# Row gather, running sum and projection: pairs of tiles handled as one, and gathers at most 7 pairs ahead

## The chip, the cores and the metric

One core of one Trainium2 chip. The metric is the device time of the core in microseconds (us), over a few executions on the same chip, and every kernel that is compared with another was timed in alternation with the kernel before on one chip. Beside it stands the span of one profiled execution. The engines go by their short names: PE multiplies matrices (PEld is its loading of weights), DVE, ACT and POOL work on elements, SP issues the stores. PSUM is the memory into which PE writes; to drain a PSUM tile is to copy it out to SBUF.

## The reference

```python
B, S, N, D = 16, 4096, 2048, 512          # x: fp32 (B,S,D); indices: (B,N), sorted, no repeats; w: fp32 (D,D)
gathered = x[np.arange(B)[:, None], indices, :]
cs = np.cumsum(gathered, axis=1)
out = np.matmul(cs, w).astype(np.float32)
```

## The kernel before

The 16 x 2,048 gathered rows are worked through as 256 tiles of 128 rows. A tile goes this way: POOL issues one indexed gather (128 rows of 2 KB, one index per partition) into a buffer; ACT casts it to fp16; PE multiplies it by a triangular matrix, which gives sums within the tile, into PSUM (`pa`); DVE adds the last column of the tile before and writes `csT`; PE multiplies that by `w16` into PSUM (`pb`); ACT or DVE drains `pb` to `ob`; SP stores two tiles at once.

```python
R, AHEAD = 2, 44
gp   = ctx.enter_context(tc.tile_pool(name="gp", bufs=AHEAD + 4))      # gathered rows: 48 tiles
g16p = ...bufs=6;  csp = ...bufs=5;  outp = ...bufs=10
psA  = ...bufs=3 (PSUM);  psB = ...bufs=5 (PSUM)
# ... (indices, w, the triangular matrix ut are loaded and built here) ...

def gather(t):
    g32s[t] = gp.tile([P, D], FP32, name="g32")
    ...
    nc.gpsimd.indirect_dma_start(out=g32s[t][:], out_offset=None, in_=x_flat,
        in_offset=bass.IndirectOffsetOnAxis(ap=ap, axis=0), element_offset=(t // NT) * S * D)

def cast(t):
    g16s[t] = g16p.tile([P, D], FP16, name="g16")
    nc.scalar.copy(out=g16s[t][:], in_=g32s.pop(t)[:])

# cumsum_tile(t): 4 matmuls into pa, then one add (or copy) on DVE into csT
# project_tile(t): 4 matmuls into pb, then
    if r == 0: nc.vector.tensor_copy(out=obs[g][:, r, :], in_=pb[:])
    else:      nc.scalar.copy(out=obs[g][:, r, :], in_=pb[:])
    # ... and after the second tile of a pair one store from SP

for t in range(FIRST, AHEAD): gather(t)          # 44 tiles of gathers before anything else
...
for t in range(T + LAG):
    if t + AHEAD < T: gather(t + AHEAD)
    if t + 1 < T:     cast(t + 1)
    if t < T:         cumsum_tile(t)
    if t >= LAG:      project_tile(t - LAG)
```

Of the kernel before, what the change touches and what calls it, by code (L numbers as in the profile page):

```python
# [1 line left out]

# [5 lines left out]

P = 128
FP32 = mybir.dt.float32  # L10
FP16 = mybir.dt.float16
U32 = mybir.dt.uint32


@with_exitstack
def kernel(
    ctx: ExitStack,
    tc: tile.TileContext,
    x: bass.AP,
    indices: bass.AP,  # L20
    w: bass.AP,
    out: bass.AP,
):
    nc = tc.nc

    B, S, D = x.shape
    N = indices.shape[1]
    R = 2
    Q = P // R
    DC = D // P  # L30
    NT = N // P
    T = B * NT
    FIRST = 2
    AHEAD = 44
    assert D == 512 and N % (R * P) == 0 and T % P == 0

    x_flat = x.rearrange("b s d -> (b s) d")

    const = ctx.enter_context(tc.tile_pool(name="const", bufs=1))
    gp = ctx.enter_context(tc.tile_pool(name="gp", bufs=AHEAD + 4))  # L40
    g16p = ctx.enter_context(tc.tile_pool(name="g16p", bufs=6))
    csp = ctx.enter_context(tc.tile_pool(name="csp", bufs=5))
    outp = ctx.enter_context(tc.tile_pool(name="outp", bufs=10))
    psA = ctx.enter_context(tc.tile_pool(name="psA", bufs=3, space=bass.MemoryType.PSUM))
    psB = ctx.enter_context(tc.tile_pool(name="psB", bufs=5, space=bass.MemoryType.PSUM))
    ctx.enter_context(tc.manual_schedule())


    idx_first = const.tile([P, FIRST, 2], U32)
    with nc.allow_non_contiguous_dma(reason="a few indices, one per partition"):  # L50
        nc.sync.dma_start(
            out=idx_first[:],
            in_=indices[0, 0 : FIRST * P].bitcast(U32).rearrange("(t p w) -> p t w", p=P, w=2),
        )

    KI = T // P
    idx_rows = indices.bitcast(U32).rearrange("b (t q) -> (b t) q", q=2 * P)
    idx64 = const.tile([P, KI, 2 * P], U32)
    for k in range(KI):
        nc.sync.dma_start(out=idx64[:, k, :], in_=idx_rows[k * P : (k + 1) * P, :])  # L60
    w32 = const.tile([P, DC, D], FP32)
    nc.sync.dma_start(out=w32[:], in_=w.rearrange("(c p) d -> p c d", p=P))


    ut = const.tile([P, R, Q], FP16)
    nc.gpsimd.memset(ut[:], 1.0)  # L66
    nc.gpsimd.affine_select(  # L67
        out=ut[:],
        in_=ut[:],
        compare_op=mybir.AluOpType.is_ge,  # L70
        fill=0.0,
        base=0,
        pattern=[[1, R], [R, Q]],
        channel_multiplier=-1,
    )
    ident = const.tile([P, P], FP32)
    make_identity(nc, ident[:])

    idxf = const.tile([P, KI, P], FP32)
    idxg = const.tile([P, KI, P], U32)  # L80
    w16 = const.tile([P, DC, D], FP16)

    g32s, g16s, cst, obs = {}, {}, {}, {}

    def gather(t):
        g32s[t] = gp.tile([P, D], FP32, name="g32")
        ap = idx_first[:, t, 0:1] if t < FIRST else idxg[:, t // P, t % P : t % P + 1]
        nc.gpsimd.indirect_dma_start(  # L88
            out=g32s[t][:],
            out_offset=None,  # L90
            in_=x_flat,
            in_offset=bass.IndirectOffsetOnAxis(ap=ap, axis=0),
            element_offset=(t // NT) * S * D,
        )

    def cast(t):
        g16s[t] = g16p.tile([P, D], FP16, name="g16")
        nc.scalar.copy(out=g16s[t][:], in_=g32s.pop(t)[:])  # L98

    def cumsum_tile(t):  # L100
        g, r = divmod(t, R)
        if r == 0:
            cst[g] = csp.tile([P, DC, R, P], FP16, name="csT")
        csT = cst[g]
        g16 = g16s.pop(t)
        pa = psA.tile([P, DC, R, Q], FP32, name="pa")
        for c in range(DC):
            nc.tensor.matmul(  # L108
                out=pa[:, c],
                lhsT=g16[:, c * P : (c + 1) * P],  # L110
                rhs=ut[:],
                start=(c == 0),
                stop=(c == DC - 1),
            )
        dst = csT[:, :, :, r * Q : (r + 1) * Q]
        if t % NT == 0:
            nc.vector.tensor_copy(out=dst, in_=pa[:])  # L117
            return
        if r == 0:
            last = cst[g - 1][:, :, R - 1, P - 1 : P]  # L120
        else:
            last = csT[:, :, R - 1, r * Q - 1 : r * Q]
        nc.vector.tensor_tensor(  # L123
            out=dst,
            in0=pa[:],
            in1=last.unsqueeze(2).broadcast_to([P, DC, R, Q]),
            op=mybir.AluOpType.add,
        )

    def project_tile(t):  # L130
        g, r = divmod(t, R)
        if r == 0:
            obs[g] = outp.tile([P, R, D], FP32, name="ob")
        csT = cst[g]
        pb = psB.tile([P, D], FP32, name="pb")
        for c in range(DC):
            nc.tensor.matmul(  # L137
                out=pb[:],
                lhsT=csT[:, c, r, :],
                rhs=w16[:, c, :],  # L140
                start=(c == 0),
                stop=(c == DC - 1),
            )
        if r == 0:
            nc.vector.tensor_copy(out=obs[g][:, r, :], in_=pb[:])  # L145
        else:
            nc.scalar.copy(out=obs[g][:, r, :], in_=pb[:])  # L147
        if r == R - 1:
            b, h = divmod(g, NT // R)
            dst = out[b, h * R * P : (h + 1) * R * P, :].rearrange("(p j) d -> p j d", j=R)  # L150
            nc.sync.dma_start(out=dst, in_=obs.pop(g)[:])

    for t in range(FIRST):
        gather(t)
    for k in range(KI):
        nc.vector.tensor_copy(out=idxf[:, k, :], in_=idx64[:, k, 0::2])  # L156
        idx_ps = psB.tile([P, P], FP32, name="idx_ps", tag="pb")
        nc.tensor.transpose(out=idx_ps[:], in_=idxf[:, k, :], identity=ident[:])  # L158
        nc.vector.tensor_copy(out=idxg[:, k, :], in_=idx_ps[:])  # L159
    for t in range(FIRST, AHEAD):  # L160
        gather(t)
    nc.scalar.copy(out=w16[:], in_=w32[:])  # L162

    LAG = R
    cast(0)
    for t in range(T + LAG):
        if t + AHEAD < T:
            gather(t + AHEAD)
        if t + 1 < T:
            cast(t + 1)  # L170
        if t < T:
            cumsum_tile(t)
        if t >= LAG:
            project_tile(t - LAG)


# [1 line left out]
_INS = ['x', 'indices', 'w']  # L178
_OUTS = [((16, 2048, 512), 'float32')]


# [23 lines left out]
```

## Time and profile before

| | before |
|---|---|
| time, median of 3 (lowest to highest) | 496.83 us (494.12 to 497.37) |
| profiled span (that run took 494.51 us) | 492.8 us |
| busy: PE / DVE / ACT / POOL | 68% / 52% / 43% / 49% of the span |
| DMA | 135.96 MB, mean 276 GB/s |
| start of the cast of tile 10 | 80.1 us |
| tiles 64 to 200, from cast to cast | 1.714 us each |

No engine is busy more than 68% of the time, so a table of totals doesn't say what the bound is. The groups of instructions show what the change touches on ACT and DVE (columns: line, engine, operation, output and input, count, then busy time and mean nanoseconds of one, then the idle time in front of them and what ended most of it):

```profile
L147 ACT COPY ob<-pb 128x512 f32<-128x512 f32 x128 | 74.9, 585 | 271.5 <-remote 147.2
...
L98 ACT CAST g<-g 128x512 f16<-128x512 f32 x256 | 145.7, 620 | 0.0
...
L145 DVE COPY ob<-pb 128x512 f32<-128x512 f32 x128 | 88.4, 691 | 76.2 <-PE pb L137 32.9
```

ACT's drains are the group to look at: 75 us of work with 271 us of standing still in front of it.

### The profile page before, as it was taken

The page shows a single profiled execution, that of the slowest core. Times are in us where ns is not written, and L with a number is a line of the kernel's source. Part 1 is how long each engine was busy: PE and PEld are TensorE (multiplying, and loading weights), DVE is VectorE, ACT ScalarE, POOL GpSimd, SP SyncE. Part 2 cuts the span into 40 slices and gives each one's busy share as a digit, 9 for nine tenths or more (in the row PEclk, how much of TensorE's full clock was granted, in tenths as well). Part 3 has the DMA queues.
Part 4 walks back from the last instruction along what each step waited for, and adds up shares of the span by engine and source line. Part 5 has one row for each costly group of instructions (what it writes and reads, how often), then busy time and mean ns, then how long its engine had stood idle before and what let it go on. Part 6 is the DMA issues. An engine that isn't in the chain of part 4 may idle for free. (4 is left out here: it accounts for less than half of the span.)

```text
span 492.8 us, 6383 instructions
## 1 busy us (share of the span) xinstructions
PE 334.8 (68%) x2050; PEld 162.4 (33%) x2050; DVE 256.3 (52%) x388; ACT 210.7 (43%) x386; POOL 243.2 (49%) x264
## 2 busy tenths in 40 slices
PE   2512012877777776788788776688886659799995
PEld 1201001433333333344333333344433324344442
DVE  1300000654665475456555664556665656577774
ACT  4100001443554454355444453535554444566663
POOL 6777771544555645564555555556555555300000
PEclk9956555787999999798888998988899997999999
DMA  7878773688888989888898988988998997855555
GB/s 235 252 206 256 208 212 122 221 293 295 304 306 299 330 321 319 291 292 282 293 320 313 345 300 301 322 274 305 308 339 310 306 335 254 319 212 211 213 211 204
DMA packets 40035, 135.96 MB, mean 276 GB/s; under 512 B 6465, under 2 KB 6721, under 8 KB 40001
## 3 DMA queue, kind: packets, MB, share of 16 engines
q0 software_dynamic: 20480, 67.13, 44.3%
q1 hardware_dynamic: 19520, 68.43, 35.0%
q8 instruction: 16, 0.26, 0.2%
q14 instruction: 19, 0.15, 0.1%
HBM read 68.42 MB, written 67.11 MB: 275 GB/s over the span
## 5 line engine op out<-in xcount | busy, mean ns | idle before, releaser
L137 PE MATMUL pb<-w,csT 128*128 128x512 f16 x1024 | 290.9, 411 | 115.9 <-DVE csT L123 72.0
L88 POOL DMA_INDIRECT g<-in_x_dram,idxg x254 | 240.0, 945 | 180.9 <-ACT g L98 122.1
L123 DVE TENSOR_TENSOR csT<-pa,csT 128x512 f16<-128x512 f32 x240 | 165.0, 688 | 138.0 <-PE pa L108 65.0
L147 ACT COPY ob<-pb 128x512 f32<-128x512 f32 x128 | 74.9, 585 | 271.5 <-remote 147.2
L137 PEld LDWEIGHTS <-csT 128*128 128x128 f16 x1024 | 91.4, 104 | 205.2 <-DVE csT L123 89.6
L98 ACT CAST g<-g 128x512 f16<-128x512 f32 x256 | 145.7, 620 | 0.0
L108 PE MATMUL pa<-ut,g 128*128 128x128 f16 x1024 | 105.9, 230 | 33.4 <-ACT g L98 22.2
L145 DVE COPY ob<-pb 128x512 f32<-128x512 f32 x128 | 88.4, 691 | 76.2 <-PE pb L137 32.9
L108 PEld LDWEIGHTS <-g 128*128 128x128 f16 x1024 | 76.9, 103 | 115.7 <-ACT g L98 57.4
L117 DVE CAST csT<-pa 128x512 f16<-128x512 f32 x16 | 11.0, 690 | 13.2 <-PE pa L108 7.6
L162 ACT CAST w<-w 128x2048 f16<-128x2048 f32 x1 | 1.9, 1897 | 6.0 <-DMA w<-in_w_dram 6.0
L158 PE MATMUL idx_ps<-ident,idxf 128*128 128x128 f32 x2 | 0.9, 461 | 4.3 <-DVE idxf L156 4.3
L88 POOL DMA_INDIRECT g<-in_x_dram,idx_first x2 | 2.0, 1022 | 1.4 <-DMA idx_first<-in_indices_dram 1.0
L156 DVE CAST idxf<-idx 128x128 f32<-128x128 uint32 x2 | 0.4, 222 | 3.5 <-DMA idx<-in_indices_dram 3.5
L158 PEld LDWEIGHTS idx_ps<-ident,idxf 128*128 128x128 f32 x2 | 0.4, 182 | 4.6 <-issue 3.8
L162 ACT ACT_TABLE_LOAD x1 | 1.3, 1283 | 0.8 <-PEq L189 0.8
L159 DVE CAST idxg<-idx_ps 128x128 uint32<-128x128 f32 x2 | 0.6, 292 | 1.2 <-PE idx_ps L158 1.2
L66 POOL MEMSET ut<- 128x128 f16 x1 | 0.2, 205 | 0.3 <-POOLq L189 0.3
L67 POOL TENSOR_SCALAR_AFFINE_SELECT ut<-ut 128x128 f16<-128x128 f16 x1 | 0.3, 292 | 0.1
masks.py:199 POOL TENSOR_SCALAR_AFFINE_SELECT ident<-ident 128x128 f32<-128x128 f32 x1 | 0.3, 292 | 0.1
L189 POOL MEMSET const-float32-0.0<- 128x1 f32 x1 | 0.1, 98 | 0.3 <-issue 0.3
masks.py:197 POOL MEMSET ident<- 128x128 f32 x1 | 0.2, 198 | 0.0
(3 smaller groups left out, 0.3 us busy)
## 6 DMA issues: line engine op xcount, KB each, us to landing
out_dram<-ob SPq DMA_DIRECT2D x128, 512.0 KB
g<-in_x_dram,idxg POOLq DMA_INDIRECT x254
w<-in_w_dram SPq DMA_DIRECT2D x1, 1024.0 KB
idx<-in_indices_dram SPq DMA_DIRECT2D x2, 128.0 KB
g<-in_x_dram,idx_first POOLq DMA_INDIRECT x2
idx_first<-in_indices_dram SPq DMA_DIRECT2D x1, 2.0 KB
```

Source lines behind the costliest of these rows:

```text
L88: nc.gpsimd.indirect_dma_start(out=g32s[t][:], out_offset=None, in_=x_flat, in_offset=bass.IndirectOffsetOnAxis(ap=ap, axis=0), element_of ...
L98: nc.scalar.copy(out=g16s[t][:], in_=g32s.pop(t)[:])
L108: nc.tensor.matmul(out=pa[:, c], lhsT=g16[:, c * P : (c + 1) * P], rhs=ut[:], start=(c == 0), stop=(c == DC - 1),)
L117: nc.vector.tensor_copy(out=dst, in_=pa[:])
L123: nc.vector.tensor_tensor(out=dst, in0=pa[:], in1=last.unsqueeze(2).broadcast_to([P, DC, R, Q]), op=mybir.AluOpType.add,)
L137: nc.tensor.matmul(out=pb[:], lhsT=csT[:, c, r, :], rhs=w16[:, c, :], start=(c == 0), stop=(c == DC - 1),)
L145: nc.vector.tensor_copy(out=obs[g][:, r, :], in_=pb[:])
L147: nc.scalar.copy(out=obs[g][:, r, :], in_=pb[:])
L156: nc.vector.tensor_copy(out=idxf[:, k, :], in_=idx64[:, k, 0::2])
L158: nc.tensor.transpose(out=idx_ps[:], in_=idxf[:, k, :], identity=ident[:])
L159: nc.vector.tensor_copy(out=idxg[:, k, :], in_=idx_ps[:])
L162: nc.scalar.copy(out=w16[:], in_=w32[:])
```

## The change

The intent: halve the number of instructions and of waits between engines by doing a cast, a drain and a PSUM tile for two tiles at once (part of an instruction's time doesn't grow with its length: ACT's cast of 512 elements took 620 ns in the trace before and its one cast of 2,048 1,897, so some 194 ns by the line through both, an estimate), and free memory by gathering fewer tiles ahead. The gathers themselves stay one per tile. Cut to its core:

```diff
-    AHEAD = 44                                   # tiles
+    AHEAD = 7                                    # pairs
-    gp = ...bufs=AHEAD + 4      # 48 buffers of one tile
+    gp = ...bufs=AHEAD + 1      # 8 buffers of a pair: 16 tiles
-    g16p 6, csp 5, psA 3, psB 5
+    g16p 3, csp 4, psA 2, psB 2                  # each now holds a pair
     def gather(g):
+        g32s[g] = gp.tile([P, R, D], FP32, name="g32")
+        for r in range(R):  # one indirect_dma_start per tile, as before
     def cast(g):
+        nc.scalar.copy(out=g16s[g][:], in_=g32s.pop(g)[:])      # [P, R, D]
     def cumsum(g):
+        # 8 matmuls into one pa, then two adds on DVE
     def project(g):
+        # 8 matmuls into one pb, then one drain:
+        if g % 4 == 3: nc.vector.tensor_copy(out=ob[:], in_=pb[:])
+        else:          nc.scalar.copy(out=ob[:], in_=pb[:])
+        # one store per pair, as before
     for g in range(G):
+        if g + AHEAD < G: gather(g + AHEAD)
+        if g + 2 < G:     cast(g + 2)            # two pairs ahead
+        if g + 1 < G:     cumsum(g + 1)
+        project(g)
```

More of the change, by code (lines that the diff above doesn't have):

```diff
@@ L32 @@
     T = B * NT
-    FIRST = 2
-    AHEAD = 44
+    G = T // R
+    GB = NT // R
+    FIRST = R
+    AHEAD = 7
     assert D == 512 and N % (R * P) == 0 and T % P == 0
@@ L39 @@
     const = ctx.enter_context(tc.tile_pool(name="const", bufs=1))
-    gp = ctx.enter_context(tc.tile_pool(name="gp", bufs=AHEAD + 4))
-    g16p = ctx.enter_context(tc.tile_pool(name="g16p", bufs=6))
-    csp = ctx.enter_context(tc.tile_pool(name="csp", bufs=5))
+    gp = ctx.enter_context(tc.tile_pool(name="gp", bufs=AHEAD + 1))
+    g16p = ctx.enter_context(tc.tile_pool(name="g16p", bufs=3))
+    csp = ctx.enter_context(tc.tile_pool(name="csp", bufs=4))
     outp = ctx.enter_context(tc.tile_pool(name="outp", bufs=10))
-    psA = ctx.enter_context(tc.tile_pool(name="psA", bufs=3, space=bass.MemoryType.PSUM))
-    psB = ctx.enter_context(tc.tile_pool(name="psB", bufs=5, space=bass.MemoryType.PSUM))
+    psA = ctx.enter_context(tc.tile_pool(name="psA", bufs=2, space=bass.MemoryType.PSUM))
+    psB = ctx.enter_context(tc.tile_pool(name="psB", bufs=2, space=bass.MemoryType.PSUM))
     ctx.enter_context(tc.manual_schedule())
@@ L81 @@
     w16 = const.tile([P, DC, D], FP16)
-    g32s, g16s, cst, obs = {}, {}, {}, {}
-    def gather(t):
-        g32s[t] = gp.tile([P, D], FP32, name="g32")
-        ap = idx_first[:, t, 0:1] if t < FIRST else idxg[:, t // P, t % P : t % P + 1]
-        nc.gpsimd.indirect_dma_start(
-            out=g32s[t][:],
-            out_offset=None,
-            in_=x_flat,
-            in_offset=bass.IndirectOffsetOnAxis(ap=ap, axis=0),
-            element_offset=(t // NT) * S * D,
-        )
-    def cast(t):
-        g16s[t] = g16p.tile([P, D], FP16, name="g16")
-        nc.scalar.copy(out=g16s[t][:], in_=g32s.pop(t)[:])
@@ L100, in cumsum_tile @@
-    def cumsum_tile(t):
-        g, r = divmod(t, R)
-        if r == 0:
-            cst[g] = csp.tile([P, DC, R, P], FP16, name="csT")
-        csT = cst[g]
-        g16 = g16s.pop(t)
-        pa = psA.tile([P, DC, R, Q], FP32, name="pa")
-        for c in range(DC):
-            nc.tensor.matmul(
-                out=pa[:, c],
-                lhsT=g16[:, c * P : (c + 1) * P],
-                rhs=ut[:],
-                start=(c == 0),
-                stop=(c == DC - 1),
-            )
-        dst = csT[:, :, :, r * Q : (r + 1) * Q]
-        if t % NT == 0:
-            nc.vector.tensor_copy(out=dst, in_=pa[:])
-            return
-        if r == 0:
-            last = cst[g - 1][:, :, R - 1, P - 1 : P]
-        else:
-            last = csT[:, :, R - 1, r * Q - 1 : r * Q]
-        nc.vector.tensor_tensor(
-            out=dst,
-            in0=pa[:],
-            in1=last.unsqueeze(2).broadcast_to([P, DC, R, Q]),
-            op=mybir.AluOpType.add,
-        )
@@ L130, in project_tile @@
-    def project_tile(t):
-        g, r = divmod(t, R)
-        if r == 0:
-            obs[g] = outp.tile([P, R, D], FP32, name="ob")
-        csT = cst[g]
-        pb = psB.tile([P, D], FP32, name="pb")
-        for c in range(DC):
-            nc.tensor.matmul(
-                out=pb[:],
-                lhsT=csT[:, c, r, :],
-                rhs=w16[:, c, :],
-                start=(c == 0),
-                stop=(c == DC - 1),
-            )
-        if r == 0:
-            nc.vector.tensor_copy(out=obs[g][:, r, :], in_=pb[:])
-        else:
-            nc.scalar.copy(out=obs[g][:, r, :], in_=pb[:])
-        if r == R - 1:
-            b, h = divmod(g, NT // R)
-            dst = out[b, h * R * P : (h + 1) * R * P, :].rearrange("(p j) d -> p j d", j=R)
-            nc.sync.dma_start(out=dst, in_=obs.pop(g)[:])
@@ L153, with gather @@
-    for t in range(FIRST):
-        gather(t)
+    g32s, g16s, cst = {}, {}, {}
+    def gather(g):
+        g32s[g] = gp.tile([P, R, D], FP32, name="g32")
+        for r in range(R):
+            t = g * R + r
+            ap = idx_first[:, t, 0:1] if t < FIRST else idxg[:, t // P, t % P : t % P + 1]
+            nc.gpsimd.indirect_dma_start(
+                out=g32s[g][:, r, :],
+                out_offset=None,
+                in_=x_flat,
+                in_offset=bass.IndirectOffsetOnAxis(ap=ap, axis=0),
+                element_offset=(t // NT) * S * D,
+            )
@@ new lines, in cast, with cumsum @@
+    def cast(g):
+        g16s[g] = g16p.tile([P, R, D], FP16, name="g16")
+        nc.scalar.copy(out=g16s[g][:], in_=g32s.pop(g)[:])
+    def cumsum(g):
+        csT = cst[g] = csp.tile([P, DC, R, P], FP16, name="csT")
+        g16 = g16s.pop(g)
+        pa = psA.tile([P, R, DC, R, Q], FP32, name="pa")
+        for r in range(R):
+            for c in range(DC):
+                nc.tensor.matmul(
+                    out=pa[:, r, c],
+                    lhsT=g16[:, r, c * P : (c + 1) * P],
+                    rhs=ut[:],
+                    start=(c == 0),
+                    stop=(c == DC - 1),
+                )
+        for r in range(R):
+            dst = csT[:, :, :, r * Q : (r + 1) * Q]
+            if g % GB == 0 and r == 0:
+                nc.vector.tensor_copy(out=dst, in_=pa[:, r])
+                continue
+            if r == 0:
+                last = cst[g - 1][:, :, R - 1, P - 1 : P]
+            else:
+                last = csT[:, :, R - 1, r * Q - 1 : r * Q]
+            nc.vector.tensor_tensor(
+                out=dst,
+                in0=pa[:, r],
+                in1=last.unsqueeze(2).broadcast_to([P, DC, R, Q]),
+                op=mybir.AluOpType.add,
+            )
@@ new lines, in project @@
+    def project(g):
+        csT = cst[g]
+        pb = psB.tile([P, R, D], FP32, name="pb")
+        for r in range(R):
+            for c in range(DC):
+                nc.tensor.matmul(
+                    out=pb[:, r],
+                    lhsT=csT[:, c, r, :],
+                    rhs=w16[:, c, :],
+                    start=(c == 0),
+                    stop=(c == DC - 1),
+                )
+        ob = outp.tile([P, R, D], FP32, name="ob")
+        if g % 4 == 3:
+            nc.vector.tensor_copy(out=ob[:], in_=pb[:])
+        else:
+            nc.scalar.copy(out=ob[:], in_=pb[:])
+        b, h = divmod(g, GB)
+        dst = out[b, h * R * P : (h + 1) * R * P, :].rearrange("(p j) d -> p j d", j=R)
+        nc.sync.dma_start(out=dst, in_=ob[:])
@@ L155 @@
+    gather(0)
     for k in range(KI):
@@ L159 @@
         nc.vector.tensor_copy(out=idxg[:, k, :], in_=idx_ps[:])
-    for t in range(FIRST, AHEAD):
-        gather(t)
+    for g in range(1, AHEAD):
+        gather(g)
+    cast(0)
     nc.scalar.copy(out=w16[:], in_=w32[:])
-    LAG = R
-    cast(0)
-    for t in range(T + LAG):
-        if t + AHEAD < T:
-            gather(t + AHEAD)
-        if t + 1 < T:
-            cast(t + 1)
-        if t < T:
-            cumsum_tile(t)
-        if t >= LAG:
-            project_tile(t - LAG)
+    cast(1)
+    cumsum(0)
+    for g in range(G):
+        if g + AHEAD < G:
+            gather(g + AHEAD)
+        if g + 2 < G:
+            cast(g + 2)
+        if g + 1 < G:
+            cumsum(g + 1)
+        project(g)
 _INS = ['x', 'indices', 'w']
```

## The prediction

Three passages are cut out of the recorded text, each where the mark stands: a paragraph of rules that no run of this case shows, a sentence that took the times of a cast and a drain of 1,024 elements from a formula, and the formula behind DVE's 1.22 us. 30 + 374 + 18 + 9 = 431 us of span and about 4 of time over it, put at 436. The times per pair that the text goes on to use (1.05 us for a cast, 1.01 for ACT's drain, 1.22 for DVE's) follow from the trace before, as estimates. ACT took 620 ns for a cast of 512 elements and 1,897 for one of 2,048: 0.83 ns an element, so 1,046 for 1,024, and at the same slope 585 + 426 = 1,011 for a drain. DVE took 292 ns to cast 128 elements out of PSUM to integers and 691 to copy 512: 1.04 ns an element, so 691 + 532 = 1,223.

To read beside it: "starts at once" is 0.05 us in the trace (a weight load of PE at 28.67 us behind an add of DVE that ends at 28.62, one at 37.53 behind a cast that ends at 37.48). The 1.73 us of a pair's projection in rival 3 is twice the 0.86 from 18.13 to 18.99 us. How late a drain may be without harm (about 1, roughly 1.2 and over 4 us, under *PE completions*) and the slack of about 0.7 us in rival 3 are estimates.

> **What bounds the kernel now.** I read the page's slices first, then three stretches, then the waits, then the timeline where an engine stood still. Time is 496.83 us; the profiled span is 492.8.
>
> The slices (four rows of the page, busy tenths in 40 slices of 12.3 us):
>
> ```profile
> PE   2512012877777776788788776688886659799995
> ...
> POOL 6777771544555645564555555556555555300000
> DMA  7878773688888989888898988988998997855555
> GB/s 235 252 206 256 208 212 122 221 293 295 304 306 299 330 321 319 291 292 282 293 320 313 345 300 301 322 274 305 308 339 310 306 335 254 319 212 211 213 211 204
> ```
>
> There are three regimes. In slices 1 to 7 POOL issues gathers almost without pause and PE nearly stands still. In the middle all run together at about 300 GB/s. In the last five slices POOL has nothing left and PE is at nine tenths. The windows give sums (columns: length, PE, PEld, DVE, ACT, POOL busy with counts, clock, DMA share, GB/s):
>
> ```profile
> 10.00:80.00 70.00, 14.62 (x64) 6.25 (x64) 7.52 (x11) 6.76 (x14) 48.52 (x52) 0.62 0.71 214
> 80.00:425.00 345.00, 259.34 (x1582) 126.30 (x1583) 198.11 (x298) 160.70 (x299) 187.09 (x198) 0.91 0.87 301
> 427.00:480.00 53.00, 50.22 (x342) 25.00 (x343) 42.18 (x64) 35.03 (x66) 0.00 (x0) 1.00 0.54 215
> ```
>
> A tile is one cast. The cast of tile 9 starts at 79.6 us, that of tile 209 at about 425: 346 us / 200 = 1.73 us a tile in the middle. In the tail, tile 214 is cast at 432.7 and tile 250 at 477.3: 44.6 / 36 = 1.24 us. The difference of 0.49 us per tile, and the 70 us in which only ten tiles or so get through, are what can be won.
>
> Why do they stand still in the first regime? No input is missing and no buffer is full. The waits (engine, line, what it waited for, total, times, longest):
>
> ```profile
> ACT ob L147 <- remote: 147.2, 28, 41.1
> POOL g L88 <- ACT g L98: 122.1, 84, 6.4
> ```
>
> "Remote" is a release whose author the profile can't match. The timeline of ACT and PE between 17 and 80 us shows who it was:
>
> ```profile
> 18.13 1.03 PE L137 MATMUL pb<-w,csT 128*128 128x512 f16 x4
> ...
> 36.38 0.58 ACT L147 COPY ob<-pb 128x512 f32<-128x512 f32 x1 [18.03 <-remote]
> ...
> 37.94 1.91 PE L137 MATMUL pb<-w,csT 128*128 128x512 f16 x4
> ...
> 79.11 0.59 ACT L147 COPY ob<-pb 128x512 f32<-128x512 f32 x1 [41.11 <-remote]
> ```
>
> The drain of tile 3 needs only the matmuls that were issued by 18.8 us, and runs at 36.4; that of tile 5 needs those of 37.9 and runs at 79.1. Both instructions wait for PE's semaphore alone. DVE's instructions behind PE are late in the same way, while what waits for ACT or DVE starts at once. So **PE's completions arrive late while POOL issues gathers back to back**: the first long row has 57 gathers from 2.9 to 74.1 us, one every 1.25 us, and the lateness of the sums grows in it from nothing (tile 3) to 3, 10, 27 and 45 us (tiles 4, 5, 6, 8; recorded end of a tile's fourth matmul to the start of DVE's add). In the middle it comes and goes:
>
> ```profile
> 248.45 0.94 POOL L88 DMA_INDIRECT g<-in_x_dram,idxg  x1 [0.30 <-issue]
> ...
> 250.62 0.58 ACT L147 COPY ob<-pb 128x512 f32<-128x512 f32 x1 [3.18 <-remote]
> ...
> 251.99 0.94 POOL L88 DMA_INDIRECT g<-in_x_dram,idxg  x1 [2.59 <-ACT g L98]
> ```
>
> Rows of 4 to 6 gathers end with PE's completions 1 to 2.4 us late, ACT's drain and the casts behind it stall, POOL waits 2.6 us for a cast to free its buffer, and all is well again. Counted tile by tile over the whole trace, 121 of the 411 matmul groups that end before 425 us have their reader start over 1 us later (some of that the reader's own queue); of the 101 after it, with no gathers left, none. I have no cause for this inside the chip, only the coincidence.
>
> [...]
>
> **The change part by part.**
>
> *Casts and drains.* ACT has 256 casts of 620 ns and 128 drains of 585. [...] Per pair ACT then has 1.05 + 0.75 x 1.01 = 1.8 us, before 1.14 (two overlapping casts) + 0.59 = 1.7: no gain there, since ACT now drains three quarters. DVE has two adds, 1.48 us, plus a quarter of a drain of some 1.22 us [...]: 1.8 instead of 2.2. Neither engine is at its limit before or after; these savings are worth nothing by themselves.
>
> *PE.* Same 2,048 matmuls. Where PE has no wait, at full clock, tile follows tile every 1.10 us (17.89 to 18.99 us). In the tail a pair takes 2.48 us, as the cast of the next tile stands behind ACT's drain and PE idles 0.3 us twice per pair. Casts two pairs ahead take that wait away: 2.2 to 2.3 us a pair, 1.13 a tile, when nothing is late.
>
> *PE completions.* Four are waited for per pair now (two sums, two projections); after it three. A late one also hurts less at ACT: casts are two pairs ahead, so a drain up to about a microsecond late no longer holds the next sum. Against it, two slots for the projections instead of five: a drain over roughly 1.2 us late stops PE, where it could be over 4 before.
>
> *Gathers.* Still 256 of 0.945 + 0.30 us: 320 us of POOL. The buffers hold 8 pairs = 16 tiles instead of 48. The opening row shrinks from 57 gathers to about 16, 20 us, ending near 23 us. Lateness begins after some 14 us of it, so it can reach only about 5 us before POOL must wait for casts. I put the cast of tile 9 at 30 us instead of 79.6: **50 us won**. The price is at the other end: gathers no longer end 47 tiles before the sums, but 16. So 31 tiles go from the 1.24 us regime to the middle's: 31 x 0.49 = **15 us given back**.
>
> *Sum.* Opening 30 us; middle 231 tiles (9 to 239); tail 16 x 1.13 = 18; end about 9 (last cast at 484.2 to 492.8 now). Fixed: 57. With the middle at its 1.73 us: 400, a span of 457. With 1.62 us, my choice: 374, span 431. The choice is a judgement: of the 0.49 us lost per tile I give back a quarter (0.11) for three completions instead of four and the slack at the casts. Time exceeds the span by about 4 us (496.83 to 492.8): **436 us**.
>
> **Rivals.**
> 1. *The middle is bound by the DMAs, and lateness only follows.* For: share 0.87 at 301 GB/s, so 346 GB/s at full share (an estimate), 1.52 us for a tile's 524 KB. Against: the 345 GB/s slice shows headroom, and the gather-only stretch is late at 214 GB/s, the tail not at 215. As a floor it gives 57 + 231 x 1.52 + 4 = 412 us; if 1.73 is already this limit, 461.
> 2. *POOL's duty sets the middle.* A freer compute side makes POOL run longer rows, and lateness rises until the rate is the old one: 461 us. For: POOL at 1.25 us a tile would be slower than PE's 1.13, so only lateness stops it.
> 3. *Two PSUM slots and pair-sized steps make late completions dearer.* The chain sum, two adds (1.5 us), projection (1.73 us) has about 0.7 us of slack; every fourth pair DVE's long drain eats it. At 1.9 us a tile: 57 + 439 + 4 = 500, no gain.
> 4. *The opening stall isn't shortened*, because lateness survives in rows of two. Then 50 us are lost again: 485. Against it: in the middle, rows of 6 cost only 2 to 3 us.
>
> **Range and chances.** The low end is the DMA floor, 410; the high end lies a little above the unchanged middle, 468. The opening's gain is the safe part; only rival 3 or 4 nearly in full would leave less than 2%. Faster 0.91, same 0.06, slower 0.03.
>
> **What would show it.** The opening row near 16 gathers, ending before 28 us; PE at work from the third slice on; cast of 1,024 near 1,046 ns and drains near 1,010 and 1,220; ACT's longest "remote" wait under 8 us instead of 41; middle windows of 1.5 to 1.75 us a tile at 300 to 345 GB/s; POOL idle only at the last 16 tiles. I am wrong if PE is idle after 30 us, if the middle is slower than 1.8 us, or if PE's waits for drained slots of pb become the largest.

## The result, and the profile after

| | before | after |
|---|---|---|
| time, median of 4 (lowest to highest) | 497.1 us (494.12 to 497.9) | 460.81 us (457.78 to 462.43) |
| ratio (95% interval) | | 0.9282 (0.923 to 0.9334): faster |
| profiled span | 492.8 us | 456.1 us |
| start of the cast of tile 10 | 80.1 us | 39.2 us |
| tiles 64 to 200 | 1.714 us each | 1.691 us each |
| last gather issued | 425.3 us | 426.4 us |

A ratio here and below is the mean time of one kernel's fast runs over the mean of the other's fast runs of the same rounds, so it is not quite the ratio of the medians. Executions over 1.5% slower than the fastest of the same kernel are left out of the means.

The slices of the kernel after (busy tenths in 40 slices, now of 11.4 us):

```profile
PE   0717865787678859776879677576776877776695
...
POOL 6764554644465555465656565456545656555300
...
DMA  7775888987998897899999999898879999888855
GB/s 233 215 249 198 305 296 301 308 317 267 338 323 298 293 361 244 321 334 328 307 348 287 330 355 307 295 309 291 320 269 333 323 332 329 293 296 306 317 218 228
```

Of the six slices before in which PE hardly worked, two are left (the first and the third). The middle looks as it did, at much the same 300 GB/s. At the end POOL has nothing left in two slices instead of five. The stretches in numbers (length, then PE, PEld, DVE, ACT and POOL busy with counts, granted clock, DMA share, GB/s):

```profile
10.00:35.00 25.00, 11.37 (x55) 5.87 (x56) 4.14 (x6) 7.97 (x7) 17.41 (x19) 0.84 0.77 237
35.00:80.00 45.00, 31.32 (x191) 15.86 (x190) 20.94 (x29) 21.39 (x23) 22.67 (x24) 0.86 0.79 276
80.00:425.00 345.00, 259.06 (x1661) 130.08 (x1658) 171.38 (x231) 174.68 (x181) 194.65 (x206) 0.93 0.90 312
```

From 80 to 425 us before issued 198 gathers and after 206: the same stretch, 4% more work. The span went down by 36.7 us, and the casts of the same tiles say where:

- to the cast of tile 10: 80.1 before, 39.2 after: **40.9 us won**;
- from there to the cast of tile 208: 344.8 before, 335.9 after: **8.9 us won**, of it the first part, where the kernel before is still in its slow opening;
- from tile 208 to the end: 67.9 before, 81.0 after: **13.1 us given back**. Gathers now end 18 tiles before the sums, not some 47.

40.9 + 8.9 - 13.1 = 36.7. The costs of the instructions came out as foreseen:

```profile
L149 ACT COPY ob<-pb 128x1024 f32<-128x1024 f32 x96 | 97.2, 1013 | 220.6 <-remote 100.2
...
L102 ACT CAST g<-g 128x1024 f16<-128x1024 f32 x128 | 130.9, 1049 | 0.0
...
L147 DVE COPY ob<-pb 128x1024 f32<-128x1024 f32 x32 | 39.2, 1224 | 23.7 <-PE pb L138 16.7
```

ACT's drains still stand behind 220 us of idle time, 100 of it put down to "remote". DVE's busy time fell from 256 to 215 us without anything to show for it. The waits (engine, line, awaited; total, times, longest):

```profile
POOL g L92 <- ACT g L102: 105.4, 39, 5.8
ACT ob L149 <- remote: 100.2, 24, 6.4
...
DVE csT L126 <- remote: 66.4, 27, 13.1
ACT ob L149 <- PE pb L138: 61.7, 32, 14.3
```

The longest wait of a drain has gone from 41.1 to 14.3 us (that one is put down to PE by name, in the opening). The kind of waiting is the old one. The timeline shows one round of it (start, duration, engine, line, operation; in brackets the idle time before):

```profile
54.06 1.89 PE L138 MATMUL pb<-w,csT 128*128 128x512 f16 x8
...
58.15 0.95 POOL L92 DMA_INDIRECT g<-in_x_dram,idxg  x1 [0.30 <-issue]
...
60.91 1.01 ACT L149 COPY ob<-pb 128x1024 f32<-128x1024 f32 x1 [6.43 <-remote]
...
63.14 0.95 POOL L92 DMA_INDIRECT g<-in_x_dram,idxg  x1 [4.04 <-ACT g L102]
```

The eight matmuls are over at 55.95. The drain that needs only them starts at 60.91, 5 us later, just after a row of eight gathers (49.4 to 59.1 us) has ended; and POOL has had to wait for the cast that stood behind that drain. Between 100 and 400 us a row of gathers (POOL pausing less than 0.9 us between them) has 2 to 8 of them in both kernels; its mean length is 4.5 before and 5.9 after.

To compare kernels I took one measure from each trace: for every add and drain, the time that its engine stood idle past the recorded end of the last matmul it needs. It includes a few tenths of ordinary delay (0.45 us at most in tiles 64 to 200 of the four runs below in which nothing is late). I call it the lateness. In tiles 64 to 200 the longest is 3.44 us before and 4.98 after; over 1 us are 36 of 272 before and 49 of 205 after.

### The profile page after: what moved, and what is told of

The parts are those of the page before. It is cut to its first block, busy times and chain, and to the rows that moved or that the text cites. A ratio compares the mean times of both kernels' runs of the same rounds, so it can differ in the third digit from the quotient of the medians.

```text
span 456.1 us, 5721 instructions
## 1 busy us (share of the span) xinstructions
PE 324.2 (71%) x2050; PEld 163.2 (36%) x2050; DVE 214.7 (47%) x292; ACT 219.6 (48%) x226; POOL 243.2 (53%) x264
## 4 chain that ended last, share of the span: by engine, by line
issue 41%; POOL 40%; DMA 8%; PE 6%; ACT 2%; DVE 2%; another core or an unknown queue 1%; SPq 0%; POOLq 0%; ACTq 0%; DVEq 0%
POOL g L92 40%; DMA g<-in_x_dram,idxg 5%; PE pb L138 4%; DMA out_dram<-ob 3%; ACT g L102 2%; PE pa L110 1%; DVE ob L147 1%; DVE csT L126 1%; DMA idx<-in_indices_dram 0%; ACT ob L149 0%; PE idx_ps L158 0%; POOLq L92 0%; SPq L152 0%; DVE idxg L159 0%
## 5 line engine op out<-in xcount | busy, mean ns | idle before, releaser
L138 PE MATMUL pb<-w,csT 128*128 128x512 f16 x1024 | 266.3, 407 | 70.3 <-DVE csT L126 49.9
L149 ACT COPY ob<-pb 128x1024 f32<-128x1024 f32 x96 | 97.2, 1013 | 220.6 <-remote 100.2
L138 PEld LDWEIGHTS <-csT 128*128 128x128 f16 x1024 | 98.2, 103 | 183.1 <-DVE csT L126 70.2
L102 ACT CAST g<-g 128x1024 f16<-128x1024 f32 x128 | 130.9, 1049 | 0.0
L110 PE MATMUL pa<-ut,g 128*128 128x128 f16 x1024 | 83.7, 228 | 52.1 <-ACT g L102 36.1
L110 PEld LDWEIGHTS <-g 128*128 128x128 f16 x1024 | 67.8, 103 | 99.6 <-ACT g L102 52.0
L147 DVE COPY ob<-pb 128x1024 f32<-128x1024 f32 x32 | 39.2, 1224 | 23.7 <-PE pb L138 16.7
```

The source lines that it names most:

```text
L102: nc.scalar.copy(out=g16s[g][:], in_=g32s.pop(g)[:])
L110: nc.tensor.matmul(out=pa[:, r, c], lhsT=g16[:, r, c * P : (c + 1) * P], rhs=ut[:], start=(c == 0), stop=(c == DC - 1),)
L138: nc.tensor.matmul(out=pb[:, r], lhsT=csT[:, c, r, :], rhs=w16[:, c, :], start=(c == 0), stop=(c == DC - 1),)
L147: nc.vector.tensor_copy(out=ob[:], in_=pb[:])
L149: nc.scalar.copy(out=ob[:], in_=pb[:])
```

## The experiments

**The theories.** *L, lateness*: indexed gathers that POOL issues close to one another hold back the signals by which PE says that matmuls are done; the opening is lost to one long row of them, and the middle settles where POOL runs until the signals come too late and then waits for a cast. The rivals: the *bytes or the DMA engines* are the limit and the lateness only follows; *any* DMA that POOL issues does it; the *prefetch depth* itself, or the *number of completions*, or the *PSUM slots and other slack*, sets the rate. Twelve kernels, in three calls of four; each call has its own runs of before, on its own chip, with medians over all of them of 490.43, 490.35 and 498.03 us. So the times in the table can't be compared across calls; the ratios can, and a ratio times 497.1 us gives a time on the scale of the result above. a_halfbytes and a_plain_pool ran twice, the others four times. Four give a wrong result; the text says which.

| kernel | time, us | ratio to before (95%) | tile 10 cast at | us per tile, 64 to 200 | longest lateness there | over 1 us |
|---|---|---|---|---|---|---|
| before | 497.1 | 1 | 80.1 | 1.714 | 3.44 | 36 of 272 |
| after | 460.81 | 0.9282 (0.923 to 0.9334) | 39.2 | 1.691 | 4.98 | 49 of 205 |
| b_depth16 | 460.08 | 0.9355 (0.9264 to 0.9446) | 38.6 | 1.703 | 2.71 | 41 of 272 |
| a_depth48 | 480.08 | 0.9792 (0.9699 to 0.9886) | 82.6 | 1.675 | 4.88 | 50 of 205 |
| a_depth8 | 445.61 | 0.9092 (0.9052 to 0.9132) | 25.2 | 1.686 | 4.90 | 46 of 204 |
| a_halfpool (wrong) | 337.85 | 0.6884 (0.6825 to 0.6944) | 22.9 | 1.257 | 0.45 | 0 of 204 |
| a_halfbytes (wrong) | 449.92 | 0.9171 (0.912 to 0.9222) | 40.0 | 1.674 | 4.97 | 45 of 204 |
| a_plain_sp (wrong) | 350.21 | 0.715 (0.7095 to 0.7206) | 23.6 | 1.301 | 0.45 | 0 of 204 |
| a_plain_pool (wrong) | 346.38 | 0.7061 (0.7024 to 0.7098) | 25.5 | 1.307 | 0.45 | 0 of 204 |
| a_gap | 420.77 | 0.8575 (0.8516 to 0.8634) | 24.0 | 1.557 | 3.88 | 56 of 204 |
| a_gap_pair | 423.31 | 0.8507 (0.8467 to 0.8547) | 25.9 | 1.519 | 3.01 | 56 of 204 |
| a_gap384 | 418.5 | 0.8421 (0.8373 to 0.8469) | 24.8 | 1.559 | 0.45 | 0 of 202 |
| b_gap | 469.39 (fast runs) | 0.9387 (0.9324 to 0.945) | 23.3 | 1.625 | 4.80 | 33 of 272 |
| b_slack | 440.81 | 0.8842 (0.8803 to 0.8881) | 26.2 | 1.621 | 5.62 | 57 of 272 |

### One part of the change alone: depth, and pairing

b_depth16 is the kernel before with 16 buffers instead of 48:

```diff
-    AHEAD = 44
+    AHEAD = 14
-    gp = ...bufs=AHEAD + 4
+    gp = ...bufs=AHEAD + 2
```

> The kernel before with nothing changed but the gathers' depth: 14 tiles ahead and 16 buffers instead of 44 and 48. Theory 1 (the whole gain is the shorter opening row of gathers, less what the shorter tail gives back; pairing is worth nothing): 455 to 466 us, opening row under 30 gathers, 1.70 to 1.73 us a tile in the middle. Rival (pairing brings the gain, depth nothing): 490 to 500 us.

Measured: ratio 0.9355. The first row has 23 gathers and ends at 31.5 us; the slices show the opening as short as after's:

```profile
PE   1618877779667777887779776977768676777895
...
POOL 6756545455555555654555565456555635556200
```

a_depth48 is the kernel after with 24 pair buffers:

```diff
-    AHEAD = 7
+    AHEAD = 23
```

> The changed kernel with 24 pair buffers (48 tiles) instead of 8. Theory 1: back to 485 to 500 us, with an opening row of over 50 gathers and PE idle for some 50 us in it. Rival (pairing brings the gain): 455 to 466 us.

Measured: ratio 0.9792, whose interval reaches over the 2% line, so its verdict is "unclear". The time of 480.08 us lies under the range; on the scale of the result, 487 us, it lies in it. The opening of the kernel before is back, with a row of 58 gathers to 75.2 us and a drain that stood idle for 40.0:

```profile
PE   0720030878769779667869777667677666699995
...
POOL 6777772556465546556556555555655555400000
```

What follows: the depth alone brings nearly the whole gain (6.5% of 7.2%), the pairing alone some 2% at 48 tiles deep. What pairing adds at 16 tiles deep isn't resolved: 0.9282 and 0.9355 come from different rounds and their intervals overlap.

a_depth8 goes on in the same direction, with 4 pair buffers:

```diff
-    AHEAD = 7
+    AHEAD = 3
```

> Correct: 4 pair buffers instead of 8. If the opening row alone is shortened again: some 8 tiles fewer in it, tail 8 tiles shorter, net 3 to 8 us faster than the changed kernel's 461, so 450 to 458 us, with the same 1.68 us a tile. If eight tiles ahead no longer cover the gathers' way to landing: slower than 461.

Measured: 445.61 us. That looks better than I expected, but before ran at 490 us in this call: on the scale of the result it is 452 us, inside the range, and by the ratios 9 us under the kernel after. The first row has 14 gathers, to 20.3 us, and tile 10 is cast at 25.2. The middle is the same 1.686. So a depth of 8, 16 or 48 tiles changes the opening and leaves the rate of the middle between 1.675 and 1.691.

This run also shows something about the lateness itself. Its first 14 gathers and those of the kernel after are issued at nearly the same times, and in both PE ends the sums of the third pair at 20.4 to 20.5 us. In a_depth8 (timeline) POOL then waits for a cast, and DVE's adds start at once:

```profile
19.40 0.95 POOL L92 DMA_INDIRECT g<-in_x_dram,idxg  x1 [0.30 <-issue]
...
20.39 1.42 DVE L126 TENSOR_TENSOR csT<-pa,csT 128x512 f16<-128x512 f32 x2 [2.47 <-issue]
...
22.15 0.95 POOL L92 DMA_INDIRECT g<-in_x_dram,idxg  x1 [1.80 <-ACT g L102]
```

In the kernel after (timeline) POOL goes on, and the same adds start 10.3 us later:

```profile
20.70 0.95 POOL L92 DMA_INDIRECT g<-in_x_dram,idxg  x1 [0.30 <-issue]
...
30.78 1.42 DVE L126 TENSOR_TENSOR csT<-pa,csT 128x512 f16<-128x512 f32 x2 [13.05 <-remote]
```

So in these two executions what holds the signal isn't the 14 gathers already issued but the ones still to come.

### What it is about the gathers

a_halfpool fetches the same bytes with half the gathers: one index per partition brings two neighbouring rows (4 KB). The rows are then not the ones asked for, so the result is wrong.

```diff
-    x_flat = x.rearrange("b s d -> (b s) d")
+    x2 = x.rearrange("b (s k) d -> (b s) (k d)", k=R)
-        for r in range(R):  # one gather per tile, in_=x_flat
+        # one gather per pair, in_=x2, out=g32s[g][:] as [P, R * D]
```

> Wrong results on purpose: one gather per pair that fetches two consecutive rows (4 KB) per index, so the same bytes with half of POOL's gathers. Theory L (POOL's gathers hold back PE's completions, and this caps the middle): completions on time, 1.2 to 1.55 us a tile, 330 to 410 us. Rival D (the middle is bound by the DMA engines at some 310 GB/s): 1.65 to 1.75 us a tile, 445 to 465 us.

Measured: 337.85 us, ratio 0.6884. The stretch from 80 to 310 us (columns as above):

```profile
80.00:310.00 230.00, 212.51 (x1462) 104.99 (x1461) 151.73 (x206) 158.66 (x160) 83.51 (x90) 1.00 1.03 418
```

418 GB/s where the kernel after has 312, PE at 92%, a tile every 1.257 us, and no add or drain in tiles 64 to 200 that is over 0.45 us late. The same loads and stores, in bytes, thus fit in far less time: neither the bytes nor the DMA engines set the 1.69 us of the middle.

a_halfbytes is the counterpart: the same number of gathers, half the bytes in each (the cast reads them twice; wrong).

```diff
-    x_flat = x.rearrange("b s d -> (b s) d")
+    x_flat = x.rearrange("b s (h d) -> (b s h) d", h=2)
-        g32s[g] = gp.tile([P, R, D], FP32, name="g32")
+        g32s[g] = gp.tile([P, R, D // 2], FP32, name="g32")
     # cast: in_=...unsqueeze(2).broadcast_to([P, R, 2, D // 2])
```

> Wrong results on purpose: every gather fetches half a row (1 KB), the cast reads it twice. POOL's gathers are as many as before, the loaded bytes half. Theory L (the number and rows of POOL's gathers cap the middle, not bytes): 1.6 to 1.75 us a tile, 430 to 462 us, completions late as in the changed kernel. Rival (bytes or DMA queues filled by the gathers hold back PE): under 400 us.

Measured: 449.92 us; the middle 1.674 us a tile, at 238 GB/s from 80 to 425 us, and the lateness of the kernel after (longest 4.97). POOL still takes 945 ns for a gather (194.65 us for 206 in that stretch). A quarter of all the traffic gone, and the rate has moved by 1%. It is the count of gathers, not their size.

a_plain_pool takes the indexing away and leaves the DMA on POOL: a plain transfer of 128 rows (every second row, so the same bytes in the same pieces; wrong).

```diff
-            nc.gpsimd.indirect_dma_start(out=g32s[g][:, r, :], ..., in_=x_flat, in_offset=...)
+            nc.gpsimd.dma_start(out=g32s[g][:, r, :], in_=x_rows[b, h * P : (h + 1) * P, :])
```

> Wrong results on purpose: the loads are plain DMAs of every second row, issued by POOL, 256 of them as before. If any descriptor work of POOL holds back PE's completions: late as in the changed kernel, 430 to 465 us, unless POOL's time for one is much shorter than 0.95 us. If only gathers through an index do it: completions on time, 335 to 360 us like the plain loads from SP.

Measured: 346.38 us, 1.307 us a tile, nothing late. The group of its loads:

```profile
L92 POOL DMA_DIRECT2D g<-in_x_dram x256 | 137.3, 537 | 185.6 <-DMA g<-in_x_dram 148.8
```

A plain DMA takes POOL 537 ns where an indexed gather takes 945. So it is not any DMA from POOL. But the expectation made an exception for a POOL time much shorter than 0.95 us, and that is what came: whether it is the index or the longer work of POOL for each gather isn't told apart. The packets don't differ: the trace has 16,384 of 4 KB and 4,096 of 4 bytes on POOL's queue in both. a_plain_sp issues the same plain transfers from SP:

```diff
-            nc.gpsimd.indirect_dma_start(out=g32s[g][:, r, :], ..., in_=x_flat, in_offset=...)
+            nc.sync.dma_start(out=g32s[g][:, r, :], in_=x_rows[b, h * P : (h + 1) * P, :])
```

> Wrong results on purpose: the loads are plain DMAs of every second row from the SP queue, same tiles, same 2 KB pieces, no work for POOL. Theory L: no completion of PE over 1 us late outside the readers' own queues, no opening stall, 1.2 to 1.55 us a tile, 320 to 410 us. Rival D: 1.65 to 1.75 us a tile, 440 to 465 us. If completions are late here too, it is the loads' traffic and not POOL that delays them.

Measured: 350.21 us, 1.301 us a tile, nothing late. It shows what the rest of the kernel can do with the gathers out of POOL's hands. What a_plain_pool leaves open: its transfers follow one another by 0.53 us, closer than any gathers, but in rows of at most eight, since POOL waits in between for earlier ones (the 148.8 us above). Whether a row of 24 or 57 plain ones would do harm isn't tested.

### The spacing of the gathers

If it is the closeness, then a pause on POOL behind each gather must help, although it makes POOL slower. a_gap puts a small memset of a spare tile (328 ns) there, which takes the spacing within a row from 1.251 to 1.443 us (the expectation has 1.6):

```diff
+    pace = const.tile([P, 256], FP32)
...
             nc.gpsimd.indirect_dma_start(...)
+            nc.gpsimd.memset(pace[:], 0.0)
```

> Correct: a memset of 128x256 on POOL behind every gather, which spaces the gathers at some 1.6 us. If it is rows of gathers without a pause that hold back PE: completions on time, 1.55 to 1.65 us a tile, 415 to 440 us, faster than the changed kernel although POOL has more to do. If only POOL's idle time or the mean rate of gathers counts: 460 to 500 us.

Measured: 420.77 us, correct, in the range of the first theory, though its "completions on time" failed. 256 more instructions on POOL, and by the two ratios to before (0.8575 and 0.9282) the time is 7.6% under that of the kernel after. The lateness isn't gone: up to 3.88 us, 56 of 204 over 1 us. a_gap384 makes the pause a little longer (spacing 1.553 us):

```diff
+    pace = const.tile([P, 384], FP32)
```

> Correct: memset of 128x384, spacing some 1.55 us. POOL alone then needs 256 x 1.55 = 397 us. If lateness is nearly gone at this spacing: 1.55 to 1.6 us a tile, 405 to 425 us, completions mostly under 2 us late. If it is not: 425 to 450 us.

Measured: 418.5 us, correct, the shortest correct time (0.8421 of before; by the ratios 9% under the kernel after). POOL's timeline, and the leading waits:

```profile
200.97 0.95 POOL L93 DMA_INDIRECT g<-in_x_dram,idxg  x1 [0.17 <-issue]
201.93 0.43 POOL L100 MEMSET pace<- 128x384 f32 x1
202.53 0.95 POOL L93 DMA_INDIRECT g<-in_x_dram,idxg  x1 [0.17 <-issue]
```

```profile
ACT g L104 <- DMA g<-in_x_dram,idxg: 140.5, 90, 3.6
PEld L112 <- ACT g L104: 135.7, 88, 6.7
DVE csT L128 <- PE pa L112: 100.4, 60, 4.3
```

The largest wait in total is now ACT's for gathered rows to land. No reader of PE in the middle is over 0.45 us late, and a tile takes 1.559 us, which is POOL's own 1.553. The bound has moved to POOL's pace, which the pause itself sets. Between 1.443 and 1.553 us the lateness vanishes. It is not that a memset stands between the gathers, since a_gap has one too: it is how long it lasts.

a_gap_pair puts the same pause in larger pieces, one memset of twice the size behind every two gathers:

```diff
+    pace = const.tile([P, 512], FP32)
     # one memset behind the two gathers of a pair
```

> Correct: the changed kernel with one memset of 128x512 (some 0.55 us) behind every two gathers instead of one of 128x256 behind each: nearly the same mean spacing (1.4 us), but pauses half as many and twice as long. If only the mean rate of gathers in a row counts: 415 to 430 us, within 2% of the other. If a gather must be followed by a pause at once: over 435 us.

Measured: 423.31 us, 1.519 us a tile in the middle, 56 of 204 over 1 us late. Against a_gap the difference lies in the opening (lateness to 5.79 us against 4.30), and the two ratios to before (0.8507 and 0.8575) have overlapping intervals: whether the pause comes behind every gather or behind every second makes no difference that these runs resolve.

b_gap puts a_gap's pause into the kernel before, 48 tiles deep:

```diff
+    pace = const.tile([P, 256], FP32)
...
         nc.gpsimd.indirect_dma_start(...)
+        nc.gpsimd.memset(pace[:], 0.0)
```

> Correct: the kernel before, 44 tiles ahead as it was, with the same memset of 128x256 behind every gather (spacing 1.445 us). If rows of gathers without a pause cause both the opening stall and the slow middle: PE is at work through the opening, 1.55 to 1.6 us a tile, 405 to 435 us, so the deep prefetch was never the fault in itself. If the depth itself stalls the opening: over 455 us.

Measured: 469.39 us (median of three fast runs), in the range of the rival (over 455 us), not of the theory. Tile 10 comes at 23.3 us, so the first stall is gone; but the opening as a whole is still slow, with tile 48 cast at 140.7 us against 94.7 in a_gap. The slices:

```profile
PE   1956563554697697778768778688785977999995
...
POOL 7888888888888768788768686888778778300000
```

With 48 buffers POOL doesn't have to wait for a cast until 125 us: the row is 85 gathers long, and late in it drains stand idle 5 to 7 us each time. In a_gap the first row is 54 gathers long and ends at 80.5 us. But depth can't be the whole reason: until 80 us POOL issues the same 54 gathers at the same times in both kernels (the 54th at 79.6), and PE already does less in b_gap. The windows (columns as above), of a_gap and then of b_gap:

```profile
10.00:80.00 70.00, 47.83 (x288) 23.71 (x288) 28.52 (x39) 32.99 (x33) 61.89 (x98) 0.93 0.88 295
...
10.00:80.00 70.00, 44.63 (x204) 19.45 (x204) 24.52 (x36) 21.13 (x39) 61.90 (x98) 0.76 0.83 263
```

288 matmuls against 204 beside the same gathers. Up to there the two differ in the pairing, with its 258 signals of PE instead of 514 over the whole kernel and its other slack; which of these it is wasn't tested, nor was the pause at 16 tiles without pairing. So a row of gathers does harm by its length at a spacing of 1.25 us (57, 24 and 14 in before, after and a_depth8) and by its density (none in a row of 113 at 1.553 us), and at 1.443 us how much harm it does depends on the kernel beside it. In tiles 64 to 200 the mean is 1.625 us a tile.

### Slack

b_slack gives b_depth16 more room everywhere else: sums four tiles ahead of projections instead of two, casts three tiles ahead, and more buffers.

```diff
-    g16p 6, csp 5, psA 3, psB 5;  LAG = R;      cast(t + 1)
+    g16p 8, csp 6, psA 4, psB 4;  LAG = 2 * R;  cast(t + 3)
```

> Correct: the kernel before at 16 tiles deep with projections four tiles behind the sums instead of two, casts three ahead instead of one, and 4 + 4 PSUM slots. If the middle settles by itself (more slack lets POOL run longer rows, which makes completions later): 1.62 to 1.72 us a tile, 443 to 462 us. If PSUM slots and slack decide what lateness costs: under 435 us.

Measured: 440.81 us, between the two ranges, and by the ratios 5.5% under b_depth16 (0.8842 and 0.9355). The middle goes from 1.703 to 1.621 us (5%), the mean row of gathers from 4.7 to 6.1, and the longest lateness from 2.71 to 5.62 us. More slack lets the kernel bear later signals; it doesn't make them earlier. In the change itself the exchange was a worse one: the longest lateness went from 3.44 to 4.98 us, for 1.3% in the rate. Several kinds of slack were changed at once, so which of them gave the 5% is not shown.

## Why the prediction was right, and which of its steps were not

436 us were predicted with a range of 410 to 468; 460.81 came. The direction was right, and so was the mechanism of the opening, from which nearly all of the gain comes. The mechanism that was to make the middle faster was not: there was a gain of 36 us, not of 61. The sum of the span was 25 us short, by these terms:

- **The middle's rate, the term that was mis-sized.** The prediction chose 1.62 us a tile for 231 tiles, 374 us. From the cast of pair 4 at 37.3 us to the last 16 tiles (430.0 us) it took 392.7, or 1.70 each: 18.7 us more. The choice gave back "a quarter (0.11) for three completions instead of four and the slack at the casts". There are two waited for per pair, not three: 258 PE instructions signal after, 514 before (two of each are transposes of indices), since both adds wait for the one signal. Even halved, the number and the slack together bought next to nothing: 1.714 and 1.691. Each late signal became later instead (longest 3.44 to 4.98 us). Rival 2 described it: a freer compute side lets POOL run longer rows, 5.9 gathers in the mean where they were 4.5, until the signals are late enough that a cast stops POOL. I had it in hand and gave it no weight in the sum. That its 461 us came out to the microsecond is luck: its middle was 7 us too long (400 for 392.7) and its opening 7 us too short. One reading behind the old rate was off as well: the cast of tile 209 starts at 427.2 us, not at about 425, which makes it 1.74 us instead of 1.73.
- **The opening**: 30 us predicted, 37.3 measured (from 79.6): 7.3 more, so 42.3 us were won where 50 had been put down. Expected were some 16 gathers in the first row; there were 24, to 32.9 us, because the first four casts freed four pair buffers while the row still ran. "PE at work from the third slice on" failed by one slice for the same reason, and the sign "I am wrong if PE is idle after 30 us" was there for some 5 us of the opening (PE stood until 32.3 us, and from 35.9 to 38.4).
- **Tail and end**: 27 us predicted, 26.1 measured: 0.9 less. The price of ending gathers later, 15 us by the prediction, was 13.1 from tile 208 on.
- **Time over span**: the 4 us came out as 4.7, but the step was a poor one: a run is only some 1.7 us longer than its own span. The rest is that both profiled runs were faster than their medians.

The terms add up: 18.7 + 7.3 - 0.9 = 25.1, and 431 + 25.1 = 456.1 us of span.

Right, and borne out by a run: that the long row of gathers causes the stall in the opening (a_depth48 brings it back); that the savings on ACT and DVE are worth little by themselves (casts 1,049 ns for 1,046, drains 1,013 and 1,224 for 1,010 and 1,220: the second 512 elements cost DVE's drain 1,224 - 691 = 533 ns; but b_depth16, with the old instructions, has a middle of 1.703 us and nearly the time of the kernel after). That close gathers are the cause, of which the prediction had only the coincidence, a_gap384 shows: the same gathers, the same depth, only further apart, and the lateness is gone. Rival 1, the DMAs as the bound, fell with a_halfpool's 418 GB/s. Rival 3 didn't happen: the middle took 1.69 us a tile, not 1.9, and the waits for slots of `pb` are not among the largest. Rival 4 held in part: the opening stall was halved, not removed, and a_depth8 with 14 gathers in its first row shows what was left to win. A sign of mine that failed: the longest "remote" wait of a drain is 6.4 us, under the 8 I named, but the longest of all is 14.3, put down to PE by name. One view alone would have missed it.

**Where the rest of the expected gain went**: into later signals. That it is the signals and not the matmuls that are late, the traces show in the events of PE's semaphore itself, which the views above don't list. In the kernel before, five groups of matmuls have recorded ends at 40.28, 71.95, 80.88, 82.58 and 83.01 us; no signal is recorded between 79.09 and 85.42 us, and then five come 0.06 us apart. The shortest group takes PE 0.39 us, so matmuls that ran late couldn't end so close together; signals that were held up and let go can. Such steps of under 0.15 us between two signals occur 46 times before and 27 times after, and never in a_gap384 and a_plain_pool. (Not every signal has a record: 435 of 514 before, 231 of 258 after.) What stays open is why close gathers delay PE's signals at all. The plain picture is a queue: something takes some 1.5 us per gather (an estimate: a spacing of 1.443 us is still late, to 3.88 us, and one of 1.553 is not, 0.45 at most), and PE's signal stands behind those already issued. It fits that half the gathers cure it (a_halfpool, 0.45 us at most), and that the last signals come some time after a row's end (1.8 us after the row of eight shown above, 3.5 after the first row of 24, 5 after the first row of 57 in the kernel before). But it doesn't fit the pair of timelines under a_depth8, where the same 14 gathers hold nothing back once POOL stops; there PE's signal rather seems to be passed over as long as more gathers come. Both are argued, not shown: no run looked inside the chip, nor told the issue on POOL from the handling of what it issues.

## What to carry to other kernels

When readers of an engine's results start late though nothing they need is missing, look at what another engine issues at that time, and count it: here the number and spacing of indexed gathers, not their bytes, set the rate (1.691 us a tile; 1.674 with half the bytes, 1.257 with half the gathers, 1.559 with the gathers 1.553 us apart). A deep prefetch is not free where the prefetching itself slows the consumers (here 16 tiles instead of 48 took 6.5% off the time); try less depth first, then an even pace with just enough room for the harm to stop (here 1.553 us from gather to gather). And where a feedback loop holds a rate (POOL runs until the others are late), easing one side of it can go into the lateness more than into the rate (1.3% from the change, 5% from b_slack): give such a rival its weight in the sum. And compare times from different chips by their ratios to a common kernel, or a difference of chips passes for a result (the medians of before were 490.35 and 498.03 us on two of them).
